# Whole weight units, regrouped gates and the experts' token modulation moved between engines in a two-model network

## The chip, the cores and the metric

The kernel is one launch on one NeuronCore of a Trainium2 chip. The metric is the device time of that launch in microseconds, the median over runs; a profiled execution has a time of its own and a span from its first to its last instruction. Engines are named as the profile names them: PE is TensorE (PEld its weight loads), DVE VectorE, ACT ScalarE, POOL GpSimd, SP SyncE, whose queue (SPq) issues the loads.

## The reference, cut to what matters

Two networks run one after the other on 256 tokens of width 1024 and 256 context tokens. The first has an attention layer and a gated linear recurrence (`hgrn2`), each with a dense feed-forward. The second has two layers, each a mixer followed by a mixture of 32 experts:

```python
# recurrence layer (cut)
q, zf, zb, i, g = jnp.split(a @ w_in, 5, axis=-1)
...                                         # two scans, forward and backward, give o
o = rms_norm(o, o_norm_w)
out = (merge_heads(o) * jax.nn.silu(g)) @ w_o     # g: the gates

# second network, per layer l of 2
x = x + g1 * mixer(...)
h2 = rmsnorm(x, norm_ffn_g[l]) * (1 + sc2) + sh2  # the tokens' modulation ahead of the experts
# layer 0: the 256 context tokens as well (512 rows), layer 1 (the last): 256 rows
x = x + g2 * hier_moe(h2, ...)

def hier_moe(xt, ...):                            # top 2 of 32 experts per token, each of width 512
    ...                                           # group softmax, top_k, weights
    hb = silu(xb @ w1[e]) * (xb @ w3[e])          # xb: the tokens of expert e, gathered
    y[tok] += weights * (hb @ w2[e])
```

All weights are float32. Those of the experts are 2 layers x 32 experts x 6 MiB = 384 MiB.

## The kernel before, in words

Features lie on the partitions (128), tokens on the free axis; `self.X` holds the running tokens as 8 chunks of 128 features. Weights come from DRAM in *units* of 128 rows x 2048 floats (1 MiB; a few are narrower). `raw` (L299) loads a unit on SP's queue as two transfers of 1024 columns each, into two tiles of a ring; the ring of the dense stages has room for 6 units (RING), in the expert stages 7 more are added (`experts`, L270). `fetch` loads units ahead of their use. SP issues in order; a transfer waits until its tile is free.

Dense products run in `linear` (L404): `split_w` cuts a unit into a high and a low part (ACT casts, DVE subtracts), and `mm3` does three products on PE. Work that must fill gaps is stepped in by hand: `step` advances one side chain by one piece after each pair of outputs, `tick` one piece of the background (the `ada` products that make the modulation vectors of later layers).

`hgrn_` (L1109) loops over four pairs of heads. For each it does five products of one unit each: two forget gates, q, the values (`token_major`) and the output gates (`take_g`), and it then appends a side chain, `hg_chain`, of 12 pieces (a preparation, 9 levels of scores, the output, a sum of squares), which is stepped under the products of the next pair of heads; the pieces that are left are done by `finish_side` at the end of that pair. After the loop the last chain is finished with one background tick a piece.

`moe` (L1455) is an expert stage. Layer 0 has 512 tokens and takes 2 experts at a time (G = 2, 64 slots each), layer 1 has 256 tokens and takes 4 (G = 4, 32 slots each; there `whole` is true). Its entry: DVE works out the router's choice in a chain of small operations that ends in `both` (L1550); PE counts positions (`pos`), DVE turns them into keys and one-hot matrices (`gather`, L1616). Meanwhile `turn` (L1474) makes token-major copies of X with the modulation applied: PE multiplies X with `dg` (the identity times the scale A, built on POOL, L1468), and adds a broadcast shift `sb`; for the first three tiles of half 0 ACT applies the token's norm y and POOL adds the shift (L1498), for the others DVE does both (L1501). In layer 0 the copies are split into a high and a low part (ACT L1507, POOL L1508). Half 0 is the first four feature chunks, half 1 the others. `gather.get` multiplies the copies with the one-hots on PE (L1647) and copies the gathered features to SBUF (L1649).

Then, for each group of G experts, `first` (L1654) does the w1 and w3 products (L1668) and `second` the w2 product (L1713); `combine` (L1733, L1734) spreads two groups' results over the tokens. Each feature chunk's product waits for the columns of the units that it reads. At the end of layer 0's stage come the loads of the next dense stage; `pair` (L384) gives high and low tiles from a small pool of their own (`early`) there, and the rest of that pool takes units of layer 1's experts ahead of time.

Of the kernel before, what the change touches and what calls it, by code (L numbers as in the profile page):

```python
# [9 lines left out]
F32 = mybir.dt.float32  # L10
# [233 lines left out]
class Net:  # L244
    def __init__(self, tc, I, out, cat, sat, ctx):
# [5 lines left out]
        self.ring = pool("ring", 2 * self.RING)  # L251
# [3 lines left out]
        self.early = None  # L255
# [13 lines left out]
    @contextmanager  # L269
    def experts(self, name, ck, ring2):  # L270
        tc = self.tc
        with tc.tile_pool(name=f"ck{name}", bufs=ck) as self.ck:
            with tc.tile_pool(name=f"ring{name}", bufs=2 * ring2) as self.ring2:
                with tc.tile_pool(name=f"r{name}", bufs=1) as self.rpool:
                    yield
# [24 lines left out]
    def raw(self, key, pool=None):  # L300
# [4 lines left out]
        n = ap.shape[-1]  # L305
        parts = []
        for i in range(0, n, 1024):
            w = min(n - i, 1024)
            t = (pool or self.ring).tile([P, 1024], F32, tag="raw", name="raw")
            self.nc.sync.dma_start(t[:, :w], ap[..., i : i + w])  # L310
            parts.append(t)
        return lambda lo, hi: parts[lo // 1024][:, lo % 1024 : lo % 1024 + hi - lo]
# [71 lines left out]
    def pair(self, pool=None):  # L384

        if pool:
            t = pool.tile([P, 1024], F32R, tag="raw", name="hl")
            return t[:, :512], t[:, 512:]
# [726 lines left out]
    def hgrn_(self, a, mod, hpool):  # L1115
# [9 lines left out]
        for hp in range(4):  # L1125
            base = hp * 5
            q = self.chunk(name="hq")
            g = self.chunk(name="hg")
# [5 lines left out]

            def take_g(k, ps):
                nc.scalar.activation(g[:, k * S : (k + 1) * S], ps[:, :S], AF.Sigmoid)
                nc.vector.tensor_tensor(g[:, k * S : (k + 1) * S], g[:, k * S : (k + 1) * S], ps[:, :S], op=ALU.mult)
# [309 lines left out]
    def moe(self, l, entry, mod, segs, sl, after):  # L1447
# [16 lines left out]
        dg, sb = {}, {}  # L1464
        for half in range(2):
# [9 lines left out]
        def turn(half):  # L1475

            for _, row in segs:
                ps = self.ps("sb")
# [8 lines left out]
            for t in range(TC):  # L1487
# [14 lines left out]
                if whole:  # L1502
                    hh[2 * t + half] = x
                    continue
# [110 lines left out]
        def gather(kt, base, width):  # L1615
# [19 lines left out]
            def get(i):  # L1635
                while len(xe) <= i:
# [102 lines left out]
        rings = [self.ring] * self.RING + [self.ring2] * (self.ring2.bufs // 2)  # L1739
# [307 lines left out]
```

## Time and profile before

| | |
|---|---|
| median of 3 runs | 2674.04 us (2669.76 to 2677.62) |
| the profiled execution | 2669.05 us, span 2667.2 us |
| PE busy | 2435.3 us, 91% of the span |
| DVE, ACT, POOL busy | 40%, 30%, 9% |
| DMA, mean | 244 GB/s; 409 GB/s in two long stretches |

The page cuts the span in 40 slices of 66.7 us:

```profile
## 2 busy tenths in 40 slices
PE   6999999999999989999998999999989988877775
POOL 1000020101111122111112000000020000000000
PEclk9999999999999999999998999999989998988987
DMA  8158442222532276557613999999934459999996
GB/s 306 64 189 289 171 172 95 95 91 83 209 113 82 80 289 226 181 173 249 237 52 135 386 409 409 408 409 409 409 132 139 147 200 409 409 409 409 409 409 250
```

Each digit is a share in tenths (9 is 90% or more). The dense stages are slices 1 to 21 and 30 to 32, layer 0's experts slices 22 to 29 (from about 1425 to 1946 us), layer 1's experts 33 to the end (from 2170 us). A matmul of two float32 operands is recorded as two instructions. The chain of work that the page follows back from the end breaks off in an empty loop at 2647 us, so the stages are read from windows, timelines and waits.

### The profile page before, as it was taken

The page shows a single profiled execution, that of the slowest core. Times are in us where ns is not written, and L with a number is a line of the kernel's source. Part 1 is how long each engine was busy: PE and PEld are TensorE (multiplying, and loading weights), DVE is VectorE, ACT ScalarE, POOL GpSimd, SP SyncE. Part 2 cuts the span into 40 slices and gives each one's busy share as a digit, 9 for nine tenths or more (in the row PEclk, how much of TensorE's full clock was granted, in tenths as well). Part 3 has the DMA queues.
Part 4 walks back from the last instruction along what each step waited for, and adds up shares of the span by engine and source line. Part 5 has one row for each costly group of instructions (what it writes and reads, how often), then busy time and mean ns, then how long its engine had stood idle before and what let it go on. Part 6 is the DMA issues. An engine that isn't in the chain of part 4 may idle for free. (4 is left out here: it accounts for less than half of the span.)

```text
span 2667.2 us, 35570 instructions
## 1 busy us (share of the span) xinstructions
PE 2435.3 (91%) x13988; PEld 1628.6 (61%) x13988; DVE 1071.7 (40%) x2220; ACT 802.5 (30%) x1430; POOL 239.2 (9%) x217
## 2 busy tenths in 40 slices
PE   6999999999999989999998999999989988877775
PEld 3556678888699958996566544544459762222212
DVE  3456243232566665555664133333344741110102
ACT  4644242222444444445442111111134521000001
POOL 1000020101111122111112000000020000000000
PEclk9999999999999999999998999999989998988987
DMA  8158442222532276557613999999934459999996
GB/s 306 64 189 289 171 172 95 95 91 83 209 113 82 80 289 226 181 173 249 237 52 135 386 409 409 408 409 409 409 132 139 147 200 409 409 409 409 409 409 250
DMA packets 181057, 649.64 MB, mean 244 GB/s; under 512 B 19985, under 2 KB 21137, under 8 KB 180753
## 3 DMA queue, kind: packets, MB, share of 16 engines
q1 hardware_dynamic: 180608, 646.21, 64.6%
q8 instruction: 114, 1.87, 0.3%
q0 software_dynamic: 272, 1.05, 0.1%
q14 instruction: 63, 0.51, 0.1%
HBM read 646.13 MB, written 1.05 MB: 243 GB/s over the span
## 5 line engine op out<-in xcount | busy, mean ns | idle before, releaser
L400 PE MATMUL ps<-h,wh 128*128 128x512 f32 (+1 forms) x1396 | 482.1, 349 | 8.7 <-ACT h L565 7.2
L401 PE MATMUL ps<-l,wh 128*128 128x512 f32 (+1 forms) x1396 | 482.8, 346 | 4.0 <-DVE l L567 3.9
L1668 PE MATMUL w<-raw,xe 128*64 128x512 f32 (+1 forms) x2040 | 416.9, 656 | 74.7 <-DMA raw<-in_moe_w_dram 70.2
L402 PE MATMUL ps<-h,wl 128*128 128x512 f32 (+1 forms) x1396 | 481.6, 346 | 3.1 <-DVE wl L330 3.1
L330 DVE TENSOR_TENSOR wl<-raw,wh 128x1024 fp32r<-128x1024 f32 x254 | 310.7, 1244 | 165.8 <-ACT wh L329 161.9
L329 ACT CAST wh<-raw 128x1024 fp32r<-128x1024 f32 (+1 forms) x258 | 258.1, 1029 | 384.4 <-PE ps L401 300.5
L1668 PEld LDWEIGHTS w<-raw,xe 128*64 128x64 f32 (+1 forms) x2040 | 128.8, 131 | 341.0 <-issue 197.2
L400 PEld LDWEIGHTS ps<-h,wh 128*128 128x128 f32 x1396 | 265.3, 191 | 59.6 <-issue 13.9
L401 PEld LDWEIGHTS ps<-l,wh 128*128 128x128 f32 x1396 | 266.8, 191 | 39.1 <-DVE l L567 6.7
L402 PEld LDWEIGHTS ps<-h,wl 128*128 128x128 f32 x1396 | 266.6, 191 | 38.4 <-DVE wl L330 3.8
L1713 PE MATMUL y<-raw,ut 128*64 128x512 f32 (+1 forms) x1024 | 225.4, 597 | 31.1 <-ACT ut L1687 15.3
L1678 DVE TENSOR_TENSOR u<-u,w 128x512 f32<-128x512 f32 x24 | 16.5, 688 | 436.0 <-PE w L1668 436.0
L1713 PEld LDWEIGHTS y<-raw,ut 128*64 128x64 f32 (+1 forms) x1024 | 65.1, 123 | 171.9 <-issue 107.0
L1724 DVE SCALAR_TENSOR_TENSOR yl<-y,st,yh 128x512 fp32r<-128x512 f32 x48 | 35.5, 750 | 294.3 <-ACT yh L1723 202.5
L583 DVE SCALAR_TENSOR_TENSOR X<-ps,mod,X 128x256 f32<-128x256 f32 x120 | 53.5, 480 | 175.5 <-PE ps L402 175.5
L400 PE MATMUL ps<-uh,wh 128*128 128x512 f32 (+1 forms) x352 | 118.3, 336 | 0.0
L401 PE MATMUL ps<-ul,wh 128*128 128x512 f32 (+1 forms) x352 | 118.3, 336 | 0.0
L402 PE MATMUL ps<-uh,wl 128*128 128x512 f32 (+1 forms) x352 | 118.3, 336 | 0.0
L630 PE MATMUL ada<-raw,cs 128*32 128x512 f32 x768 | 112.3, 606 | 2.7 <-DMA raw<-in_ada_dram 2.6
L964 POOL TENSOR_TENSOR ul<-u,uh 128x512 fp32r<-128x512 f32 (+1 forms) x44 | 74.9, 1702 | 414.4 <-ACT uh L963 414.4
L960 DVE TENSOR_TENSOR u<-u,ps 128x512 f32<-128x512 f32 (+1 forms) x44 | 24.4, 555 | 206.1 <-PE ps L402 199.5
L1723 ACT ACTIVATE yh<-y,st 128x512 fp32r<-128x512 f32 x48 | 32.3, 686 | 237.4 <-PE y L1713 237.0
(372 smaller groups left out, 3498.8 us busy)
## 6 DMA issues: line engine op xcount, KB each, us to landing
raw<-in_moe_w_dram SPq DMA_DIRECT2D x766, 512.0 KB, 10.2
raw<-in_ada_dram SPq DMA_DIRECT2D x192, 512.0 KB, 5.4
raw<-in_ffn_dram SPq DMA_DIRECT2D x128, 512.0 KB, 4.6
raw<-in_hg_in_dram SPq DMA_DIRECT2D x40, 512.0 KB, 4.8
raw<-in_od_in_dram SPq DMA_DIRECT2D x24, 512.0 KB, 9.7
raw<-in_ev_in_dram SPq DMA_DIRECT2D x10, 512.0 KB, 6.3
raw<-in_mla_o_dram SPq DMA_DIRECT2D x8, 512.0 KB, 7.0
raw<-in_hg_o_dram SPq DMA_DIRECT2D x8, 512.0 KB, 9.9
```

What stands on the lines that cost most here:

```text
L329: self.nc.scalar.copy(h[:, c], rc)
L330: eng.tensor_tensor(l[:, c], rc, h[:, c].bitcast(F32), op=ALU.subtract)
L400: mm(out, w[0], a[0], start=start, stop=False)
L401: mm(out, w[0], a[1], start=False, stop=False)
L402: mm(out, w[1], a[0], start=False, stop=stop)
L583: self.nc.vector.scalar_tensor_tensor(x, ps[:, cs], self.m(mod, m, row)[:, k : k + 1], x, op0=ALU.mult, op1=ALU.add)
L630: nc.tensor.matmul(ps[32 * j : 32 * j + 32, :], self.cs[:, blk, k, :], r(j * 512, (j + 1) * 512), start=k == 0, stop=k == NC - 1,)
L964: nc.gpsimd.tensor_tensor(lo[:, :n], u, h[:, :n].bitcast(F32), op=ALU.subtract)
L1668: end = nc.tensor.matmul(ps[x * cap : (x + 1) * cap, :], xk[:, off + x * cap : off + (x + 1) * cap], wc[x], start=k == 0, stop=k == NC - 1,)
L1713: nc.tensor.matmul(ys[nh][x * cap : (x + 1) * cap, :], ut[:, hc * P + x * cap : hc * P + (x + 1) * cap], wc[x], start=hc == 0, stop=hc == 3,)
L1723: ACT.activation(yh[:], ys[nh][:], AF.Copy, scale=sw)
L1724: V.scalar_tensor_tensor(yl[:], ys[nh][:], sw, yh[:].bitcast(F32), op0=ALU.mult, op1=ALU.subtract)
```

## The change

- `raw` loads a unit with one transfer of 2048 columns into one tile; the rings count whole units (6, 7 and 5 tiles of 2048 columns in place of twice as many of 1024). The high and low tiles of `pair` are halves of such a tile.
- In `hgrn_` the gates' four units leave the loop; one `linear` over the four follows it, before the last chain is finished.
- In `moe` with 512 tokens (layer 0): `dg` is built on ACT, four operations of 128 columns a tile, inside `turn`; norm and shift are applied by DVE for every tile, issued after `both` (half 0) or after the one-hots (half 1); the low part of tiles 2 and 3 of half 0 is made on DVE after the one-hots (`late`), the rest stays on POOL.
- In `moe` with 256 tokens (layer 1): X is only transposed, both halves at once, and multiplied by the norm on ACT; there is no `dg`, no `sb`, nothing on POOL. Scale and shift are applied when the gathered features are copied out, ACT and DVE by turns.

```diff
@@ class Net, pools
-        self.ring = pool("ring", 2 * self.RING)
+        self.ring = pool("ring", self.RING)
...
@@ raw
-        n = ap.shape[-1]
-        parts = []
-        for i in range(0, n, 1024):
-            w = min(n - i, 1024)
-            t = (pool or self.ring).tile([P, 1024], F32, tag="raw", name="raw")
-            self.nc.sync.dma_start(t[:, :w], ap[..., i : i + w])
-            parts.append(t)
-        return lambda lo, hi: parts[lo // 1024][:, lo % 1024 : lo % 1024 + hi - lo]
+        t = (pool or self.ring).tile([P, 2048], F32, tag="raw", name="raw")
+        self.nc.sync.dma_start(t[:, : ap.shape[-1]], ap)
+        return lambda lo, hi: t[:, lo:hi]
...
@@ pair
-            t = pool.tile([P, 1024], F32R, tag="raw", name="hl")
+            if not self.halves:
+                t = pool.tile([P, 2048], F32R, tag="raw", name="hl")
+                self.halves = [t[:, 1024:], t[:, :1024]]
+            t = self.halves.pop()
...
@@ hgrn_
-            self.linear([("hg_in", base + 4)], 8, 2, a, lat, take_g)
-            G.append(g)
             self.finish_side()
             self.side.append(self.hg_chain(hp, q, fc, kc, fl, kl, V, O, sums, mk, zero))
+
+        def take_g(k, ps):
+            if k % 2 == 0:
+                G.append(self.chunk(name="hg"))
+            g, ks = G[-1], slice(k % 2 * S, (k % 2 + 1) * S)
+            nc.scalar.activation(g[:, ks], ps[:, :S], AF.Sigmoid)
+            nc.vector.tensor_tensor(g[:, ks], g[:, ks], ps[:, :S], op=ALU.mult)
+
+        self.linear([("hg_in", 5 * hp + 4) for hp in range(4)], 8, 2, a, lat, take_g)
         self.finish_side(1)
...
@@ moe, turn
+            if whole:
+                for i in range(0 if half else 2 * TC):
+                    t, h = divmod(i, 2)
+                    tp = self.ps("htp")
+                    for c in range(4):
+                        x = self.X[:, h * 4 + c, sl.start + t * P : sl.start + (t + 1) * P]
+                        nc.tensor.transpose(tp[:, c * P : (c + 1) * P], x, ident)
+                    x = hh[i] = self.chunk(name="tx")
+                    ACT.activation(x[:], tp[:], AF.Copy, scale=y[:, t : t + 1])
+                return
             for _, row in segs:
                 d = dg[row, half] = self.chunk(name="dg")
-                nc.gpsimd.tensor_tensor(
-                    d[:].rearrange("p (k e) -> p k e", k=4),
-                    ident.unsqueeze(1).broadcast_to([P, 4, P]),
-                    A[:, row * 8 + half * 4 : row * 8 + half * 4 + 4].unsqueeze(2).broadcast_to([P, 4, P]),
-                    op=ALU.mult,
-                )
+                for c in range(4):
+                    k = row * 8 + half * 4 + c
+                    ACT.activation(d[:, c * P : (c + 1) * P], ident, AF.Copy, scale=A[:, k : k + 1])
...
-                if half == 0 and t < 3:
-                    ACT.activation(x[:], tp[:], AF.Copy, scale=y[:, t : t + 1])
-                    nc.gpsimd.tensor_tensor(x[:], x[:], sb[row][:], op=ALU.add)
-                else:
-                    with tc.issue_after(hot_ins[-1] if half else both_ins[-1]):
-                        V.scalar_tensor_tensor(x[:], tp[:], y[:, t : t + 1], sb[row][:], op0=ALU.mult, op1=ALU.add)
+                with tc.issue_after(hot_ins[-1] if half else both_ins[-1]):
+                    V.scalar_tensor_tensor(x[:], tp[:], y[:, t : t + 1], sb[row][:], op0=ALU.mult, op1=ALU.add)
...
-                nc.gpsimd.tensor_tensor(lo[:], x[:], h[:].bitcast(F32), op=ALU.subtract)
+                rest = lambda eng, lo=lo, x=x, h=h: eng.tensor_tensor(lo[:], x[:], h[:].bitcast(F32), op=ALU.subtract)
+                if half or t < 2:
+                    rest(nc.gpsimd)
+                else:
+                    late.append(rest)
...
@@ gather.get
-                    nc.scalar.copy(x[:], ps[:])
+                    if not whole:
+                        ACT.copy(x[:], ps[:])
                     for j in range(per):
-                        xe.append(x[:, j * width : (j + 1) * width])
+                        o, s = (v[:, j * width : (j + 1) * width] for v in (x, ps))
+                        scale, shift = mod_of(len(xe))
+                        if whole and j % 2:
+                            V.tensor_scalar(o, s, scale, shift, op0=ALU.mult, op1=ALU.add)
+                        elif whole:
+                            ACT.activation(o, s, AF.Identity, bias=shift, scale=scale)
+                        xe.append(o)
...
             if g == 0:
+                with tc.issue_after(hot_ins[-1]):
+                    for rest in late:
+                        rest(V)
                 turn(1)
```

## Rows read from the trace of the kernel before

**Rows 1.** Windows: inside layer 0's and layer 1's experts; busy us, granted clock, DMA share, GB/s.

```profile
1500.00:1900.00 400.00, 388.12 (x1976) 196.55 (x1974) 125.91 (x284) 50.38 (x82) 0.00 (x0) 1.00 1.03 409
2210.00:2600.00 390.00, 296.66 (x1519) 96.18 (x1522) 41.95 (x111) 25.28 (x41) 0.00 (x0) 0.90 1.03 409
```

**Rows 2.** Timeline of PE in layer 0: start, us, line, count, [idle before, releaser].

```profile
1712.32 13.95 PE L1668 MATMUL w<-raw,xe 128*64 128x512 f32 x64
...
1771.94 7.89 PE L1668 MATMUL w<-raw,xe 128*64 128x512 f32 x34
...
1785.52 3.65 PE L1668 MATMUL w<-raw,xe 128*64 128x512 f32 x14 [1.47 <-DMA raw<-in_moe_w_dram]
```

**Rows 3.** Waits of PE in layer 1's experts: us in total, times, longest.

```profile
PE w L1668 <- DMA raw<-in_moe_w_dram: 66.7, 47, 2.2
```

**Rows 4.** Page, parts 2, 3, 6: packets by size, instruction queues, two kinds of load.

```profile
DMA packets 181057, 649.64 MB, mean 244 GB/s; under 512 B 19985, under 2 KB 21137, under 8 KB 180753
...
q8 instruction: 114, 1.87, 0.3%
...
q14 instruction: 63, 0.51, 0.1%
...
raw<-in_moe_w_dram SPq DMA_DIRECT2D x766, 512.0 KB, 10.2
...
X<-in_x_dram SPq DMA_DIRECT2D x1, 2048.0 KB, 9.7
```

**Rows 5.** Windows in the first microseconds, while X is being loaded.

```profile
8.00:9.00 1.00, 0.00 (x0) 0.00 (x0) 0.00 (x0) 0.00 (x0) 0.00 (x0) 1.00 0.96 410
...
4.00:9.00 5.00, 0.00 (x0) 0.00 (x0) 0.78 (x4) 0.99 (x2) 0.00 (x0) 1.00 1.03 411
```

**Rows 6.** DVE by line and shape, 1424 to 1442 us: busy, mean ns, idle before.

```profile
L1529 DVE TENSOR_TENSOR r<-eq,r 128x128 f32<-128x128 f32 x2 | 2.3, 1140 | 0.1
L1569 DVE TENSOR_TENSOR tmp<-r,cst 128x128 f32<-128x128 f32 x2 | 1.6, 814 | 0.0
L1537 DVE TENSOR_TENSOR r<-L,r 128x32 f32<-128x32 f32 x4 | 1.6, 461 | 0.0
L1526 DVE TENSOR_TENSOR eq<-r,r 128x128 f32<-128x128 f32 x2 | 1.6, 800 | 0.1
L1527 DVE TENSOR_TENSOR eq<-eq,cst 128x128 f32<-128x128 f32 x2 | 1.5, 756 | 0.0
...
L519 DVE TENSOR_SCALAR rq<-rq 128x4 f32<-128x4 f32 x1 | 1.0, 961 | 0.0
...
L1545 DVE SCALAR_TENSOR_TENSOR r<-r,r 128x128 f32<-128x128 f32 x1 | 0.3, 292 | 0.0
```

**Rows 7.** The same view of ACT, POOL and DVE, 1424 to 1456 us.

```profile
L1508 POOL TENSOR_TENSOR tl<-tx,th 128x512 fp32r<-128x512 f32 x8 | 10.3, 1285 | 11.0 <-ACT th L1507 10.8
...
L1501 DVE SCALAR_TENSOR_TENSOR tx<-htp,rq,sb 128x512 f32<-128x512 f32 x5 | 3.7, 740 | 0.0
...
L1497 ACT ACTIVATE tx<-htp,rq 128x512 f32<-128x512 f32 x3 | 2.1, 684 | 0.3 <-PE htp L1492 0.3
```

**Rows 8.** Waits, 1424 to 1456 us: layer 0's entry on PE.

```profile
PE pos L1554 <- DVE r L1550: 8.7, 1, 8.7
```

**Rows 9.** DVE by line and shape, 2170 to 2182 us: layer 1's entry.

```profile
L1527 DVE TENSOR_TENSOR eq<-eq,cst 128x8 f32<-128x8 f32 x1 | 1.2, 1177 | 0.0
L1529 DVE TENSOR_TENSOR r<-eq,r 128x8 f32<-128x8 f32 x1 | 1.0, 987 | 0.0
```

**Rows 10.** Timeline of PE: layer 1's first product.

```profile
2189.78 3.64 PE L1668 MATMUL w<-raw,xe 128*32 128x512 f32 x32 [0.68 <-ACT xe L1649]
```

**Rows 11.** Window around it: busy us, granted clock, DMA share, GB/s.

```profile
2190.00:2200.00 10.00, 10.00 (x86) 4.27 (x82) 0.00 (x0) 0.59 (x2) 0.00 (x0) 1.00 0.76 265
```

**Rows 12.** Timeline of PE in the recurrence, at the end of a pair of heads.

```profile
811.43 1.95 PE L1051 MATMUL att<-qt,kt 128*128 128x128 f32 x16
```

**Rows 13.** ACT in the recurrence, 720 to 1010 us: by line and shape.

```profile
L1031 ACT COPY qt<-Qf 128x256 f32<-128x256 f32 x32 | 13.4, 419 | 12.5 <-DVE Qf L1019 9.8 <-DVE Qf L1023 2.7
```

More of the change, by code (lines that the diff above doesn't have):

```diff
@@ L254, in __init__ @@
         self.dpool = self.begin.enter_context(tc.tile_pool(name="dpool", bufs=1))
-        self.early = None
+        self.early, self.halves = None, []
         self.ready, self.cut, self.background, self.side, self.due = {}, {}, [], [], []
@@ L272, in experts @@
         with tc.tile_pool(name=f"ck{name}", bufs=ck) as self.ck:
-            with tc.tile_pool(name=f"ring{name}", bufs=2 * ring2) as self.ring2:
+            with tc.tile_pool(name=f"ring{name}", bufs=ring2) as self.ring2:
                 with tc.tile_pool(name=f"r{name}", bufs=1) as self.rpool:
@@ L1127, in hgrn_ @@
             q = self.chunk(name="hq")
-            g = self.chunk(name="hg")
             fc, kc, fl, kl = ([self.chunk(name=nm) for _ in range(2)] for nm in ("fc", "kc", "fl", "kl"))
@@ L1133, in take_q @@
                 nc.scalar.copy(q[:, k * S : (k + 1) * S], ps[:, :S])
-            def take_g(k, ps):
-                nc.scalar.activation(g[:, k * S : (k + 1) * S], ps[:, :S], AF.Sigmoid)
-                nc.vector.tensor_tensor(g[:, k * S : (k + 1) * S], g[:, k * S : (k + 1) * S], ps[:, :S], op=ALU.mult)
             def take_z(d):
@@ L1463, in moe, with turn @@
         ident = self.c("ident")
-        dg, sb = {}, {}
-        for half in range(2):
+        dg, sb, late = {}, {}, []
+        mod_of = lambda k: (A[:, segs[0][1] * 8 + k : segs[0][1] * 8 + k + 1], self.m(mod, 3, segs[0][1])[:, k : k + 1])
+        def turn(half):
+            if whole:
[8 more added lines that the diff above has]
+                return
             for _, row in segs:
                 d = dg[row, half] = self.chunk(name="dg")
-                nc.gpsimd.tensor_tensor(
-                    d[:].rearrange("p (k e) -> p k e", k=4),
-                    ident.unsqueeze(1).broadcast_to([P, 4, P]),
-                    A[:, row * 8 + half * 4 : row * 8 + half * 4 + 4].unsqueeze(2).broadcast_to([P, 4, P]),
-                    op=ALU.mult,
-                )
-        def turn(half):
-            for _, row in segs:
+                for c in range(4):
+                    k = row * 8 + half * 4 + c
+                    ACT.activation(d[:, c * P : (c + 1) * P], ident, AF.Copy, scale=A[:, k : k + 1])
                 ps = self.ps("sb")
@@ L1495, in turn @@
                 x = self.chunk(name="tx")
-                if half == 0 and t < 3:
-                    ACT.activation(x[:], tp[:], AF.Copy, scale=y[:, t : t + 1])
-                    nc.gpsimd.tensor_tensor(x[:], x[:], sb[row][:], op=ALU.add)
-                else:
-                    with tc.issue_after(hot_ins[-1] if half else both_ins[-1]):
-                        V.scalar_tensor_tensor(x[:], tp[:], y[:, t : t + 1], sb[row][:], op0=ALU.mult, op1=ALU.add)
-                if whole:
-                    hh[2 * t + half] = x
-                    continue
+                with tc.issue_after(hot_ins[-1] if half else both_ins[-1]):
+                    V.scalar_tensor_tensor(x[:], tp[:], y[:, t : t + 1], sb[row][:], op0=ALU.mult, op1=ALU.add)
                 h = self.chunk(F32R, name="th")
@@ L1738, in moe @@
         nxt = [0]
-        rings = [self.ring] * self.RING + [self.ring2] * (self.ring2.bufs // 2)
+        rings = [self.ring] * self.RING + [self.ring2] * self.ring2.bufs
         extra = int(self.early is not None)
         if self.early:
-            rings = [self.early] * (self.early.bufs // 2) + rings
+            rings = [self.early] * self.early.bufs + rings
         def static(g):
@@ L1918, in run @@
             r = self.full_rstd([self.X[:, k, al] for k in range(NC)], T)
-        with self.tc.tile_pool(name="early", bufs=2 * self.EARLY) as self.early:
+        with self.tc.tile_pool(name="early", bufs=self.EARLY) as self.early:
             with self.dense("b", 28):
```

## The prediction

> **What bounds the kernel now.** I read the page's slices first, then windows inside the two expert stages, then who PE waits for, and last the timelines of the two entries. The page's slices show PE nearly always busy in the dense stages and a flat 409 GB/s in the two expert stages. In the dense stages PE sets the time and the loads run ahead, so the number of loads there costs nothing. The expert stages differ from each other. In layer 1 the loads run at 409 GB/s throughout while PE is busy 297 us of 390 [rows 1], and PE waits 66.7 us for units in its w products alone [rows 3]: the loads set the time. In layer 0 both are full: PE is busy 388 of 400 us at the same 409 GB/s [rows 1]. There I read PE's timeline. Four experts take PE from 1712.32 to 1771.94, 59.6 us [rows 2]; their 24 units of 1,048,576 bytes take 24 x 2.564 = 61.5 us at 409 GB/s. The loads are 1.9 us a round slower, and the 13 units that are loaded ahead hide this until 1772 us. Then 64 products that took 13.95 us end at 1785.52 + 3.65, after 17.2 us [rows 2]: 3.3 us of waiting, followed by three more such stretches to the stage's end with some 1.8 us each, 8.7 us together. At both entries DVE's routing chain is on the path: PE waits 8.7 us for it in layer 0 [rows 8].
>
> **The change, part by part.** The sums are made against the profiled execution, 2669.05 us (span 2667.2 and 1.9 around it). It lies 5.0 below the median of the runs, which I add at the end.
>
> *Whole units.* A row of a unit in DRAM is 8 KB, and before it was fetched in two pieces of 4 KB. Does a longer row move faster? The only load in this trace with rows over 4 KB is X's, 128 rows of 16 KB. Its rows were not cut: 181057 - 180753 = 304 packets have 8 KB and more, of which 114 + 63 are instruction loads at most, so at least 127 are X's [rows 4]. The rate I take per busy DMA engine, because engines were idle in part: 409 / 1.03 = 397 in the steady stream [rows 1]; while X came in, 411 / 1.03 = 399 over five microseconds, and 410 / 0.96 = 427 in the last one that X fills [rows 5]. So 16 KB rows need 0.5% to 7.0% less engine time. Were this a fixed cost of a packet, 16 KB saves three packets of four and 8 KB two, two thirds of it: 0.3% to 4.7%. Both rows are short and early, neither is nearer to a steady stream, so I take the middle, 2.6%: 420 GB/s, 2.497 us a unit.
>
> [...]
>
> Layer 1: 192 units less 18 loaded ahead, 174 x 2.564 = 446 us, become 174 x 2.497 = 434.4: **-11.6** (-1.3 to -20.9). PE's 76% leaves it room to follow. Layer 0: 24 x 2.497 = 59.9 us against PE's 59.6. The drift falls from 1.9 to 0.3 us a round, some 2 us over the stage, and the stock that lasted 4.4 rounds was worth 4.4 x 1.9 = 8.4. A whole unit takes something from that stock: its first columns are there one half transfer (1.28 us) later, and its tile comes free one half later, 2.6 together. What is left still covers the drift, so PE's waiting of 8.7 us goes nearly away: **-8** (from +1.2, when the rate gains 0.3%, to -8.7); after that PE itself is the bound, and no faster load brings more. At the very end of layer 1 the last w2 unit comes as a whole: 16 more of the products are done after it has landed, at 3.64 / 32 = 0.114 us [rows 10]: **+1.8**. SP issues half as many loads, which nothing waits for. A ring holds as many units as before; a few narrow units take a whole tile, in stages where PE sets the time: nothing.
>
> *Entry of layer 0.* Seven kinds of DVE operations in the chain before `both` stand beside POOL's work, and five of them take two to four times what an operation of their size takes alone: L1529 1.140 us, L1569 0.814, L1526 0.800, L1527 0.756, against 0.292 for L1545 of the same 128x128 [rows 6]. The excess is 2 x (0.848 + 0.522 + 0.508 + 0.464) = 4.7; L1537 and L519, smaller and so bounded by the same 0.292, add 4 x 0.169 + 0.669 = 1.3. After the change POOL has nothing to do before `both`, so the chain is 6.0 us shorter. What comes back: three more tiles on DVE at 0.740 [rows 7] fall into its wait for PE's positions; the two low parts moved to DVE, at most 0.74 each, come between the one-hots and the next tiles, and the first gather needs them. Until now that gather came right behind PE's second half of `turn`, so part of the 1.5 us is hidden there: +1 (0.5 to 1.5). ACT builds `dg` in eight operations of 128 columns a half; a 512-column one takes 0.684 [rows 7], so they take between a quarter and the whole of that, 1.4 to 5.5 us a half. I take them at nothing, since ACT waits for `sb` from PE in that time and the multiplications behind it are needed only after `both`; if that cover is gone, up to 3 us return. POOL's two low parts (1.285 us each [rows 7]) stay ahead of the one-hots' end. Sum **-5** (-1.5 to -5.5). Next in line is then the copy of the gathered features on ACT, behind the casts of half 1. As PE or the loads bound the stage from there on and both start with the first product, what the entry gains is kept.
>
> *Entry of layer 1.* The chain has two such operations, 1.177 and 0.987 us for 128x8 [rows 9]: 1.6 us at least; PE's second half of `turn` ahead of the first gather is gone too, so the first product starts 1.6 to 3.5 us sooner. It is the loads that matter here, which idle (1 - 265/409) x 10 = 3.5 us around that product [rows 11], waiting for it to free a tile. A whole unit is freed at the end of the 32 products, 3.64 us [rows 10], its first half was freed midway, 1.8 sooner. So loading resumes between 0.2 later and 1.7 sooner: **-1**. The copies with scale and shift are split between ACT and DVE, which are nearly idle in that stage.
>
> *Gates.* Each pair's chain loses the gates' product, under which its score levels 7 and 8 ran without a gap (1.95 us for the 16 instructions [rows 12]). What must be ready for them are four copies a level on ACT, 0.419 each [rows 13]: 2 x 4 x 0.419 = 3.35 us a pair, which stands open if nothing else is ready, and nothing if the next pair's first product, whose weights are cut in time, moves in front. Three pairs: 0 to +10; **+3**, nearer to the lower end, as products and chain pieces are interleaved there already. The last chain now runs under the gates' 23 us; the eight background ticks that filled it move to later ticks: nothing.
>
> **Sum.** -11.6 - 8 + 1.8 - 5 - 1 + 3 = -20.8: 2648.2 against the profiled execution, **2653** against the median.
>
> **The rivals.**
> *Rows of 8 KB move no faster* (or the unit is still cut into 4 KB). [...] Against it: X's uncut rows and the last microsecond. Then layer 1 gives -1.3, layer 0 +1.2, the rest stays: +1.2 - 1.3 + 1.8 - 5 - 1 + 3 = -1.3, or 2673. Chance 0.16, no change that can be told.
> *Longer rows move slower.* Twice the bytes are under way at a time, up to 8 transfers of 1 MiB, and an engine is held twice as long by a row. At an unchanged 409 the sum is +2.6 + 1.8 - 5 - 1 + 3 = +1.4. Then both stages are bound by the loads, 174 + 179 units; from 0.019 us a unit more, 406 GB/s, it is slower by over 0.3%. At 400 GB/s: 353 x 0.057 = 20, plus 1.4: 2696. Against it: no window of rows 1 or 5 is below 397 per busy engine. Chance 0.04.
> *The rate rises, but the moved work shows.* All three chains stand open (+10 in place of +3) and ACT's `dg` delays layer 0 (+3): -20.8 + 10 = -11, or 2663. For it: the chain's copies have no other cover by the program's order. Chance 0.12.
> The forecast has 0.68.
>
> **How the numbers follow.** 0.3% of 2674 us, 8 us, is about what a measurement of this kernel tells from no change. Faster: 0.68 + 0.12 = 0.80; same 0.16; slower 0.04. With the best ends, -20.9 - 8.7 + 1.8 - 5.5 - 1.7 + 0 = -35, the time is 2639. The other end of the range takes in the third rival and reaches toward the first: 2670.
>
> **What would show it.** Right: units of 1 MiB and packets of 8 KB, about 420 GB/s in both stages; no wait of w for a load in layer 0, PE's round still 59.6 us; PE's wait for the routing chain in layer 0 down from 8.7 to about 3 us, with no DVE operation of 128x128 over 0.3 us before `both`; layer 1's stream some 12 us shorter. Wrong: 409 GB/s as before (first rival), less (second), new waits of PE for ACT's `qt` or `kt` copies at the ends of pairs or for `dg` (third).

## The result, and the profile after

The median falls from 2674.06 to 2644.32 us (four runs of each; after 2642.53 to 2645.18): 0.9889 of the time before, 95% interval 0.9871 to 0.9906. The prediction, 2653 with a range of 2639 to 2670, holds the time and its sign, but it is 9 us too high. The profiled execution after took 2644.89 us (span 2643.1), 24.2 below that of before.

What the change does to the loads is on the page: half as many packets, one load of 1 MiB for a unit, and in the experts' slices 419 to 420 GB/s. The first line shows all transfers by the size of their packets (of 93495 packets only 16784 are now below 8 KB, against 180753 of 181057 in [rows 4]). The second is the group of layer 0's and 1's products, with the idle time ahead of them. The third is the expert units' loads with size and time to landing.

```profile
DMA packets 93495, 649.52 MB, mean 246 GB/s; under 512 B 10256, under 2 KB 11408, under 8 KB 16784
...
L1679 PE MATMUL w<-raw,xe 128*64 128x512 f32 (+1 forms) x2040 | 406.2, 634 | 76.2 <-DMA raw<-in_moe_w_dram 72.7
...
raw<-in_moe_w_dram SPq DMA_DIRECT2D x383, 1024.0 KB, 19.9
```

Windows inside the two expert stages of the changed kernel, columns as in [rows 1]. The rate is 10 to 11 GB/s higher in both, and PE's share of layer 0 rises from 388.12 to 390.89 of 400 us.

```profile
1490.00:1890.00 400.00, 390.89 (x2003) 198.89 (x2003) 128.72 (x290) 52.20 (x84) 0.00 (x0) 1.00 1.01 419
2190.00:2580.00 390.00, 291.92 (x1565) 99.39 (x1557) 51.47 (x129) 27.29 (x47) 0.00 (x0) 0.93 1.01 420
```

PE's timeline in layer 0, where [rows 2] had the first wait for a unit. The four-expert round is again 1766.32 - 1706.70 = 59.62 us, but the stretch that took 17.2 us takes 13.95 now, and no wait follows.

```profile
1706.70 13.95 PE L1679 MATMUL w<-raw,xe 128*64 128x512 f32 x64
...
1766.32 13.95 PE L1679 MATMUL w<-raw,xe 128*64 128x512 f32 x64
```

At layer 0's entry PE's wait for the routing chain is 2.8 us, against 8.7 [rows 8]. The wait for the gathered features was there before (3.1 us, now 2.4); the one for ACT's `dg` is new:

```profile
PE pos L1558 <- DVE r L1554: 2.8, 1, 2.8
...
PE w L1679 <- ACT xe L1654: 2.4, 1, 2.4
...
PE htp L1499 <- ACT dg L1484: 1.9, 1, 1.9
```

DVE there, by line and shape: the operations that [rows 6] shows at 0.76 to 1.14 us take 0.28 to 0.29.

```profile
L1533 DVE TENSOR_TENSOR r<-eq,r 128x128 f32<-128x128 f32 x2 | 0.6, 292 | 0.1
...
L1573 DVE TENSOR_TENSOR tmp<-r,cst 128x128 f32<-128x128 f32 x2 | 0.6, 282 | 0.0
```

**Where the time went, stage by stage.** I took the start of the same PE product at each boundary in both timelines. The table gives each stage's length less that of before, in us, for the changed kernel and a second set of runs of it, and for eight of the kernels that follow (each is introduced below). The boundaries in the kernel before: the norm ahead of the recurrence at 703.88, the next norm at 1019.14, the router's transposed logits at 1424.85, layer 0's first `w` at 1455.41, the norm behind it at 1950.91, layer 1's logits at 2170.92, its first `w` at 2189.78, the last norm at 2652.08.

| kernel | to 704 | 704-1019 | 1019-1425 | entry 0 | layer 0 | 1951-2171 | entry 1 | layer 1 | end |
|---|---|---|---|---|---|---|---|---|---|
| changed | +6.7 | -6.7 | -1.0 | -4.7 | -6.8 | 0.0 | -2.3 | -10.2 | +1.0 |
| changed, again | +8.9 | -7.7 | -0.7 | -4.4 | -6.7 | -1.0 | -2.3 | -10.0 | +0.9 |
| whole units alone | +8.3 | +1.5 | -0.8 | 0.0 | -8.4 | -1.0 | +0.1 | -10.4 | -0.2 |
| gates alone | +5.4 | -1.7 | +0.1 | -0.3 | -0.4 | +0.3 | +0.1 | +0.2 | 0.0 |
| two transfers | +0.9 | -2.6 | +0.6 | -5.0 | +3.3 | +0.5 | -2.3 | +0.9 | -0.2 |
| one transfer, 4 KB | +6.8 | -6.0 | +0.4 | -4.5 | +2.6 | +0.7 | -2.4 | +1.1 | +0.5 |
| first cast | +4.7 | -6.7 | -0.6 | -4.4 | -6.5 | -1.0 | -2.3 | -9.9 | +0.8 |
| ticks early | +9.0 | +7.6 | -3.7 | -4.9 | -8.1 | +0.3 | -2.3 | -9.4 | +0.9 |
| both mended | -1.5 | -6.6 | +0.4 | -3.6 | -5.6 | +0.1 | -2.3 | -10.2 | +1.0 |
| ticks late | +3.3 | -3.2 | +13.0 | -5.2 | -5.8 | +0.1 | -2.3 | -10.2 | +1.0 |

Two stages went as no term of the sum had it: the start, some 7 us worse, and the recurrence with its output product, some 7 us better. They hide each other in the total.

**The start.** PE's first dense product begins at 46.81 instead of 38.59. The view is PE's timeline, before and after:

```profile
35.93 0.66 PE L643 MATMUL adat<-cst,adae 128*128 128x128 f32 x4 [0.69 <-ACT adae L640]
38.59 0.73 PE L400 MATMUL ps<-h,wh 128*128 128x512 f32 x2 [2.00 <-ACT h L565]
```

```profile
37.54 1.12 PE L641 MATMUL adat<-cst,adae 128*128 128x128 f32 x4 [0.71 <-ACT adae L638]
46.81 0.80 PE L398 MATMUL ps<-h,wh 128*128 128x512 f32 x1 [8.16 <-ACT wh L324]
```

It waits 8.16 us for ACT's cast of the first weights, 6.2 more than it waited there before; another 1.6 of the delay were lost ahead of that (37.54 against 35.93). ACT's timeline shows that cast as the first operation behind `adae` before, and as the one behind thirteen operations of the modulation after, with ACT busy from 39.17 almost throughout:

```profile
35.77 1.05 ACT L329 CAST wh<-raw 128x1024 fp32r<-128x1024 f32 x1
```

```profile
39.17 0.60 ACT L555 ACTIVATE t<-t,mod,modA 128x256 f32<-128x256 f32 x1 [1.68 <-DVE modA L527]
...
45.73 1.03 ACT L324 CAST wh<-raw 128x1024 fp32r<-128x1024 f32 x1
```

**The recurrence.** PE has 4.1 us of new waits at the ends of two pairs. But the windows (before, then after; the recurrence with its chain, and the attention) show 64 products fewer in the first stretch and 60 more in the second, which is nevertheless 1.0 us shorter: its granted clock is 1.00 in place of 0.97, and PE idles 5.5 us of it instead of 8.9. The first stretch is 4.2 us shorter; the other 2.4 us of the stage's gain lie in the output product behind it.

```profile
PE att L1049 <- ACT kt L1032: 4.1, 4, 1.1
```

```profile
703.88:979.08 275.20, 265.91 (x1840) 229.84 (x1836) 177.92 (x350) 132.30 (x274) 58.63 (x67) 0.99 0.42 147
...
1222.97:1386.34 163.37, 154.44 (x893) 99.58 (x889) 101.53 (x243) 81.31 (x169) 30.49 (x44) 0.97 0.51 183
```

```profile
710.57:981.54 270.97, 259.13 (x1776) 228.84 (x1772) 179.94 (x348) 133.43 (x276) 59.28 (x67) 0.99 0.33 120
...
1222.99:1385.36 162.37, 156.90 (x953) 98.31 (x950) 103.63 (x247) 81.64 (x170) 30.75 (x44) 1.00 0.63 233
```

PE's waits in the attention show which ones went, before and then after. The longest single one was not for a softmax result but for ACT's copy `adae` at the end of a bank of background products:

```profile
PE adat L643 <- ACT adae L640: 3.1, 1, 3.1
PE tp L714 <- ACT p L704: 3.1, 3, 2.4
```

```profile
PE tp L712 <- ACT p L702: 1.8, 1, 1.8
...
PE adat L641 <- ACT adae L638: 0.7, 1, 0.7
```

### The profile page after: what moved, and what is told of

Read it like the earlier page. It is cut to its first block, busy times and chain, and to the rows that moved or that the text cites. A ratio compares the mean times of both kernels' runs of the same rounds, so it can differ in the third digit from the quotient of the medians.

```text
span 2643.1 us, 34246 instructions
## 1 busy us (share of the span) xinstructions
PE 2411.1 (91%) x13956; PEld 1622.6 (61%) x13956; DVE 1077.7 (41%) x2243; ACT 807.1 (31%) x1447; POOL 224.4 (8%) x204
## 2 busy tenths in 40 slices
DMA packets 93495, 649.52 MB, mean 246 GB/s; under 512 B 10256, under 2 KB 11408, under 8 KB 16784
## 5 line engine op out<-in xcount | busy, mean ns | idle before, releaser
L1679 PE MATMUL w<-raw,xe 128*64 128x512 f32 (+1 forms) x2040 | 406.2, 634 | 76.2 <-DMA raw<-in_moe_w_dram 72.7
```

The lines of the kernel that those rows point to most:

```text
L1679: end = nc.tensor.matmul(ps[x * cap : (x + 1) * cap, :], xk[:, off + x * cap : off + (x + 1) * cap], wc[x], start=k == 0, stop=k == NC - 1,)
```

## The experiments

**Is it the row, the transfer or the tile?** My theory: the 8 KB row. Rivals: the transfer of 1 MiB (half as many transfers and completions), or something in the whole tiles. The first kernel has the loads' part of the change and nothing else (`raw`, the rings, `pair`).

> The kernel before with the whole units alone: one 1 MiB transfer a unit, whole tiles; gates and modulation as before. If the loads' part does what the traces suggest, the stream of layer 1 runs at 420 GB/s and gives 10 us, PE's waits for units in layer 0 vanish and give 7, and the start is some 7 us later, because the first weights come as a whole unit and ACT's cast of them stands behind the modulation in its queue: -10, about 2664 in the median. The rival is that the start has another cause (the gates or the modulation's order): then the first dense product starts at 39 us as before, and the time is 17 below, 2657.

2657.31 us, 0.9943 of before (0.9927 to 0.9960). The median is the rival's figure, but the trace decides against it: the start is 8.3 later, with the same wait of PE, 8.15 us. Both expert stages gain at least what they gain in the whole change (-8.4 and -10.4; some 1.7 of the 8.4, by an estimate of 10 x 0.17, would be the granted clock of layer 0's first 10 us, 1.00 where the kernel before and the changed one have 0.83), the entries nothing. So the loads' part brings both the gain in the experts and the loss at the start.

The second kernel cuts each unit's load in two again, into the same whole tile:

```
-        self.nc.sync.dma_start(t[:, : ap.shape[-1]], ap)
+        n = ap.shape[-1]
+        for i in range(0, n, 1024):
+            c = slice(i, min(i + 1024, n))
+            self.nc.sync.dma_start(t[:, c], ap[..., c])
```

> The changed kernel, but every unit is fetched by two transfers of 1024 columns into its whole tile: rows of 4 KB, slots and all else as changed. If the length of a row sets the rate, both expert stages fall back to 409 GB/s: layer 1 gives back 10 us and layer 0 about 7. The first half unit lands some 2.5 us earlier and its cast stands ahead of the modulation in ACT's queue, so the start gains 7: together 10 slower than the changed kernel, 2654. If the whole tile or anything but the row were behind the rate, it stays 420 and the time is 7 below the changed kernel, 2637.

2665.44 us, 0.9981 (0.9971 to 0.9991). The third keeps one transfer of 1 MiB for an expert unit but has the unit in DRAM as two blocks of 1024 columns, so that a row is 4 KB:

```
-        a[f"moe_{n}"] = np.ascontiguousarray(w.reshape(2, 32, 2, P, 2048))
+        a[f"moe_{n}"] = np.ascontiguousarray(w.reshape(2, 32, 2, P, 2, 1024).transpose(0, 1, 2, 4, 3, 5))
...
+            self.nc.sync.dma_start(t[:].rearrange("p (h c) -> p h c", h=2), ap.rearrange("h p c -> p h c"))
```

> The changed kernel, but the experts' units lie in DRAM as two blocks of 1024 columns and come by one transfer of 1 MiB with 4 KB rows; the other units keep their 8 KB rows. If the length of a row sets the rate: 409 GB/s in both expert stages, packets of 4 KB, 17 us slower than the changed kernel, 2661. If the size of the transfer sets it (half as many transfers and half as many completions): 420 GB/s and 2644.

2666.96 us, 0.9984 (0.9974 to 0.9993). The windows of the two kernels, layer 0 and layer 1 of each:

```profile
1490.00:1890.00 400.00, 387.34 (x1970) 195.22 (x1970) 126.91 (x288) 50.34 (x83) 0.00 (x0) 1.00 1.03 409
2210.00:2600.00 390.00, 295.54 (x1490) 97.47 (x1479) 48.77 (x121) 25.19 (x42) 0.00 (x0) 0.90 1.03 409
```

```profile
1500.00:1900.00 400.00, 387.72 (x1970) 196.13 (x1970) 126.45 (x284) 50.57 (x82) 0.00 (x0) 1.00 1.03 409
2210.00:2600.00 390.00, 287.68 (x1498) 96.18 (x1494) 48.81 (x121) 25.31 (x42) 0.00 (x0) 0.93 1.03 409
```

409 in all four. Transfers of 512 KB and of 1 MiB ran at the same rate with rows of 4 KB, and the whole tile changed nothing: what separates these 409 from the 419 to 420 of the changed kernel is the row's length. The two kernels' totals missed my figures (2654 and 2661). In both, layer 0 came out some 3 us worse than before and layer 1 some 1 us, and not level. Layer 0's loss fits the 2.6 us which the prediction charged a whole tile for being filled and freed later; what splits it I haven't tried. With two transfers the recurrence, too, is 4.1 us worse than in the changed kernel: PE waits 6.7 us there for ACT's `rh`, as in the kernel with the gates alone below. Two transfers also give the start back: first dense product at 39.93, wait 2.00.

**What the start costs, and why.** Theory: the place of the first cast in ACT's queue. Rival: the whole unit lands later. Here I only fix the first cast ahead of the modulation in ACT's queue (the lines in `split_w` that note this cast as `self.first` are left out).

```
-            a = self.modulated(m0, "norm1_0", 0, 1, whole, al, r=r)
+            self.first, key = None, ("mla_in", 0)
+            self.cut[key] = self.split_w(key)
+            with self.tc.issue_after(self.first):
+                a = self.modulated(m0, "norm1_0", 0, 1, whole, al, r=r)
```

> The changed kernel once more, to stand beside the three that follow: 0.989 of the kernel before.

> The changed kernel with one thing more: ACT's modulation of the first features is issued behind ACT's first cast of the first dense weights, instead of ahead of it. If the 8.2 us that PE waits at 38.7 us come from the order in ACT's queue, the cast starts when the whole unit has landed, near 39 us, and PE's first dense product near 41.5 in place of 46.8: 5 us sooner, of which 4 or more are still there at 700 us, 2640. If they come from the whole unit's later landing, the product still starts at 45 us or later: 2644.

The changed kernel again: 2645.10 us, 0.9889 (0.9872 to 0.9905). With the first cast ahead: 2640.48, 0.9870 (0.9853 to 0.9886), 4.6 less on the same chip. Its cast (ACT's timeline) and first dense product (PE's):

```profile
39.42 1.99 ACT L324 CAST wh<-raw 128x1024 fp32r<-128x1024 f32 x2 [1.51 <-DMA raw<-in_mla_in_dram]
```

```profile
42.28 1.22 PE L400 MATMUL ps<-h,wh 128*128 128x512 f32 x2 [3.20 <-ACT h L565]
```

The cast begins when the unit has landed, 6 us sooner than in the changed kernel. PE's wait is 3.2 us, against 2.0 with two transfers and 8.2 with the cast behind: of the 6.2 us the queue's order accounts for 5.0, and the later landing, with the modulation now behind the cast, for at most 1.2.

> The changed kernel, but the three units of the first dense weights come by two transfers of 1024 columns each, into whole tiles. The order that is worked out at build time then has the first cast ahead of the modulation, and the first half lands 2.5 us sooner than the whole: first dense product near 40 us as in the kernel with two transfers everywhere (39.9), PE's wait before it 2.0 in place of 8.2, and 6.7 us less at 700 us: 2638. If the start is lost to something else (the constants' whole tile, the units loaded ahead), the wait stays: 2644.

2643.51 us, 0.9882 (0.9865 to 0.9899); only these three units are cut, by `w = 1024 if key[0] == "mla_in" else n` in `raw`. First product at 42.52, wait 3.44; at 704 us it stands 3.9 better than the changed kernel's second set, but 1.6 of that is lost again in the recurrence and 2.6 in the attention (165.2 us against 162.7; in its first 30 us the granted clock is 0.89 against 1.00). The figure of 2638 was too good. The start also varies by itself: the kernel with the gates alone has the start of before, word for word, and its first dense product was at 42.45. Over the profiles, eight kernels with an early first cast (the one before among them) reach the norm at 704 us between 1.5 sooner and 5.4 later than before, six with the late one between 6.7 and 9.0 later. The means are 2.3 and 7.9: the late cast costs some 5.6 us, of which the medians of the two kernels on one chip show 4.6.

**The gates and the ticks.** The gates' part of the diff alone (`hgrn_`), on the kernel before:

> The kernel before with the regrouped gates alone. The prediction on record gives +3 (0 to +10). The trace after the change suggests otherwise: the stretch from the recurrence's start (704 us) to 1386 us is 7.7 us shorter, with 4.1 us of new waits of the score products for ACT's copies, but eight background ticks moved from the recurrence into the attention of 1223 to 1386 us, where they fill PE's waits and keep the granted clock at 1.00 (0.97 before). If that is the gates' doing, the time is 2666 (-8). If it came from the whole units in those stages instead, the gates alone cost the 4 us of new waits: 2678.

2671.91 us, 0.9992 (0.9981 to 1.0003): no change. The 4.1 us of waits are there, the 64 products have moved too, but the recurrence with its output gains 1.7 us and not 6.7. The difference is one wait: PE waits 6.7 us for ACT's `rh` at the recurrence's end, and 2.1 in the changed kernel. ACT's timeline shows why, here with the gates alone and then changed:

```profile
976.51 1.04 ACT L329 CAST wh<-raw 128x1024 fp32r<-128x1024 f32 x1 [1.29 <-DMA raw<-in_hg_o_dram]
977.57 1.28 ACT L468 ACT_TABLE_LOAD   x1
...
984.06 0.62 ACT L679 CAST rh<-r 128x512 fp32r<-128x512 f32 x1 [1.74 <-DVE r L471]
```

```profile
976.66 1.28 ACT L466 ACT_TABLE_LOAD   x1
...
978.76 1.99 ACT L324 CAST wh<-raw 128x1024 fp32r<-128x1024 f32 x2 [0.17 <-DMA raw<-in_hg_o_dram]
980.87 0.62 ACT L677 CAST rh<-r 128x512 fp32r<-128x512 f32 x1
```

With half loads the cast of the next weights stands ahead of the norm's last activation (L468) and waits for its load there; with whole units it stands behind it (L466). The late activation makes 2.3 us of the 4.6; as much again goes to DVE, where the low parts `wl` of the weights cast so early stand between the three last steps of the norm. It is the start's mechanism with the other sign.

Then the ticks. Theory: the eight background ticks (one bank, 64 products) that left the recurrence are the gain. I put eight back, in one block ahead of the last chain's remaining pieces and not, as before, one after each piece:

```
+        self.tick(8)
         self.finish_side(1)
         R = self.rows_rstd(sums, 3)
```

> The changed kernel with eight background ticks (one bank of a later block's modulation, 64 products and about 9 us of PE) put back into the recurrence, as before. If their move is what gave 7 us there, the recurrence is 9 us longer, and the attention of 1223 to 1386 us loses their 8 us of products but gets back PE's waits for the softmax (3.1 and 1.6 us) and the lower granted clock (0.97): 6 slower than the changed kernel, 2650. If their place is without effect: 2644.

2657.93 us, 0.9941 (0.9924 to 0.9957): 12.8 above the changed kernel, twice what I expected. The same two stretches:

```profile
712.91:994.40 281.49, 266.21 (x1829) 231.20 (x1826) 179.53 (x350) 131.94 (x274) 59.35 (x67) 0.99 0.38 140
...
1239.00:1399.21 160.21, 151.50 (x892) 97.75 (x889) 101.32 (x243) 81.05 (x169) 31.96 (x44) 0.99 0.49 185
```

The recurrence has 53 products more than in the changed kernel and is 281.49 - 270.97 = 10.5 us longer; the attention has 61 fewer and is only 162.37 - 160.21 = 2.2 shorter. So the bank costs some 10 us in the recurrence and about 2 in the attention, 8 net. Of the 10, PE's busy time is 266.21 - 259.13 = 7.1; the rest is idle time, 2.3 of it waits for the bank's own loads. Behind it the output product is 3.8 us longer (41.4 against 37.6): PE is busy 1.9 longer, at a granted clock of 0.84 against 0.91, and idles 1.9 longer, since it waits 4.8 us for ACT's cast of the weights, which in this kernel stands behind the four casts of `h`. So the 12.8 us are not the ticks' own price alone. PE's waits, in the recurrence and then from 700 to 1425 us:

```profile
PE ada L628 <- DMA raw<-in_ada_dram: 2.3, 2, 2.0
```

```profile
PE ps L398 <- ACT wh L324: 4.8, 1, 4.8
```

Against the kernel before, the stretch from 704 to 1425 us is 7.6 - 3.7 = 3.9 us longer. That is near the 4.1 us of waits for `kt`, but as it holds these other waits too, it doesn't show by itself what the regrouping costs if the ticks stay.

The opposite, no ticks in the last chain (with the first cast ahead):

```
-        self.finish_side(1)
+        self.finish_side()
         R = self.rows_rstd(sums, 3)
```

> The changed kernel with the first cast ahead of the modulation (2640.5 so far), and the last pair's chain without background ticks: the ticks that stood there (some 2 units of 8 products and the rest of a bank) move into the attention as well. If a tick is worth the wait that it lies under, and not more, the recurrence loses their products, gets back waits of about 1 us at the last chain's levels, and the attention, where PE idles only 5.5 of 162 us now, has to add most of them to its time: no gain, 2640 to 2645. If ticks in the recurrence cost their whole time whatever lies beside them, as the eight that were put back did, the time falls by 4 or more: 2636 or less.

2656.66 us, 0.9938 (0.9914 to 0.9962), 16 above the kernel with the first cast: worse than either figure. The recurrence has 32 products fewer and is yet 275.39 - 270.95 = 4.4 us longer, with a wait of 6.9 us for ACT's copy `adae` at the end of a bank, and the attention is 174.81 - 162.78 = 12.0 us longer than with the first cast alone, most of it a wait for the same copy. In ACT's queue it stands behind the norm's last cast in the one place and behind the casts of the next weights and features in the other. So this run doesn't decide between its two figures: what it shows is the price of a bank that ends at such a place. PE's waits, in the recurrence and then from 1230 us on:

```profile
PE adat L643 <- ACT adae L640: 6.9, 1, 6.9
```

```profile
PE adat L643 <- ACT adae L640: 10.5, 2, 9.8
```

**The entry of layer 0.** One part undone: `dg` on POOL again.

```
-                for c in range(4):
-                    k = row * 8 + half * 4 + c
-                    ACT.activation(d[:, c * P : (c + 1) * P], ident, AF.Copy, scale=A[:, k : k + 1])
+                nc.gpsimd.tensor_tensor(d[:]..., ident..., A[:, row * 8 + half * 4 : ...]..., op=ALU.mult)
```

> The changed kernel with one part of the change undone: the diagonals `dg` of layer 0 are built by POOL again, all else as changed. If DVE's operations are slowed by a POOL operation beside them, the two that fall under the first half's `dg` (L519 and the first L521-type of the rsqrt) take 0.96 us again in place of 0.16, PE's wait for the routing chain grows from 2.8 us by 1.6, and the second half's `dg` (2 us) slows some one-hots: the first product of layer 0 is 1.5 to 3 later, 2647. If ACT's `dg` costs as much where it stands now (PE waits 1.9 us for it in the second half), the two cancel: 2645.

2645.59 us, 0.9905 (0.9884 to 0.9926): no difference. The premise did not come about: only two diagonals instead of four are built at the start, and POOL is through with them at 1422.65 + 2.04 = 1424.69, before the operations that had been slowed; the chain's wait on PE stays at 2.9 us. The later ones do fall beside DVE. POOL's timeline, then DVE's:

```profile
1422.65 2.04 POOL L1482 TENSOR_TENSOR dg<-cst,modA 128x512 f32<-128x512 f32 x2 [50.09 <-PE s L2013]
...
1438.36 2.04 POOL L1482 TENSOR_TENSOR dg<-cst,modA 128x512 f32<-128x512 f32 x2
```

```profile
1436.71 0.16 DVE L1603 TENSOR_SCALAR r<-r 128x4 f32<-128x4 f32 x1
...
1439.41 1.01 DVE L1603 TENSOR_SCALAR r<-r 128x4 f32<-128x4 f32 x1
```

The same line takes 0.16 us with POOL idle and 1.01 with POOL busy, and ends at 1440.42, just as POOL does (1438.36 + 2.04 = 1440.40). That POOL's other operations slowed the chain before the change is read from such overlaps and from [rows 6]; no run puts only them back.

Next, ACT's diagonals of the second half moved into its idle 5.6 us in the first half's `turn`, with the first cast ahead:

```
                 ACT.copy(sb[row][:], ps[:])
+            if half == 0:
+                for _, row in segs:
+                    diagonals(row, 1)
             for t in range(TC):
```

> The changed kernel with the first cast ahead of the modulation (as in the run on the first cast, 4.6 below the changed kernel) and with ACT's diagonals of the second half issued in the first half's `turn`, where ACT idles for 5.6 us while the routing chain runs. If PE's wait of 1.9 us for `dg` was on the path of layer 0's entry, the first product is up to 1.9 sooner and, PE being the bound of that stage, 1.9 is kept: 2639. If the gather's one-hots come no sooner than before, only the first cast counts: 2640.5.

2641.24 us, 0.9892 (0.9869 to 0.9915): 4.4 below the run with `dg` on POOL, in the same set, which is what the first cast alone gave, and no more. PE's wait of 1.9 us for `dg` is gone, and the wait for the gathered features takes its place (4.7 instead of 2.4):

```profile
PE w L1688 <- ACT xe L1663: 4.7, 1, 4.7
```

Last, background ticks at each pair's end on top of that (`finish_side(1)` in the loop of `hgrn_` for `finish_side()`):

> As the run with both mended, and in addition the end of each pair's chain takes a background tick at each step, which fall beside the four waits of 1.0 us that the regrouped gates opened. If the waits are filled, 4.1 us of PE's waits for `kt` go and two ticks a pair, some 1.1 us each, come from the stretches behind: at best 4 less than with both mended, 2635; if the ticks only take the place of others that lay under waits later, no gain or up to 3 more.

2653.49 us, 0.9937 (0.9912 to 0.9962), 12 more than without them and worse than any figure I had. The waits for `kt` are gone, but the recurrence is 290.04 - 271.05 = 19.0 us longer than with both mended: it has 95 products more, 15.6 us of PE's busy time, and another long wait for the copy at a bank's end, behind the norm in ACT's queue (PE's waits there; 1.2 us with both mended):

```profile
PE adat L643 <- ACT adae L640: 11.9, 3, 9.5
```

Filling four waits of 1.0 us with ticks was no bargain here.

The best version is the changed kernel with its first cast ahead of the modulation: 2640.5 against 2645.1 us.

## Why the prediction was right in sign and range, and 9 us too high

*The rate.* The step that carried most, 420 GB/s for 8 KB rows, is exact, and its assumption (a fixed cost of a packet) fits what was measured. The exactness is in part luck: 2.6% was the middle of 0.3% to 4.7%, taken because neither of two short rows was nearer. The evidence for the assumption: in the packets' records of the trace the median is 161 ns for 4096 bytes before and 313 for 8192 after, against 322 for two, and 611 for the 16384 of X's rows in both, against 644 for four: 9 and 11 ns for each packet saved. The price at which rivals one and two would have decided, 409 or less, was seen only in the kernels with 4 KB rows.

*Layer 1.* -11.6 + 1.8 = -9.8 predicted, -10.2 measured. The +1.8 was no cost: PE's last stretch of `y` products behind the last wait is 20 products in 3.62 us in both timelines, so before the change, too, most of the last unit's products came after it had landed. That leaves the -11.6 too large by 1.4, for which no run here shows the reason.

*Layer 0.* -8 predicted, -6.8 measured. The waits for units are gone and the round is 59.6 us, as foretold. Of the 8.7 us that I read as waiting, the last 1.8 were none: the stretch at the stage's end, split by the combination's products, is there unchanged after. I had counted four stretches by their length, and should have looked for the releaser in each.

*Entry of layer 0.* -5 predicted, -4.7 (again -4.4) measured. The chain shrank more than my 6.0: from the logits to PE's positions it is 1433.21 - 1423.87 = 9.3 us instead of 16.8 (PE waits 8.7 of them, [rows 8]), 7.4 less, and 2.7 came back, not 1. My 6.0 had left out one operation, L521 (0.96 us beside POOL at 1426.44, 0.16 later in the same chain). `dg` was not hidden as I had it, since PE waits 1.9 us for it, but that wait isn't on the path: with it removed the product starts no sooner. What is late next is the copy of the gathered features, as the prediction said.

*Entry of layer 1.* -1 predicted, -2.3 in every kernel that has that part. My bound of -1.7 was too narrow: it held the loads' resumption to be the limit, worked out from the time at which a unit is freed. The gain is kept: this entry and layer 1 together give -12.5, against -10.3 with whole units alone.

*Gates.* Their own price was about right: +3 predicted, within 0 to +10, and 4.1 us of waits for `kt` measured, at two pairs' ends (2.1 us each, not 3.35) and not at the third. The step that failed is the clause behind it, "the eight background ticks that filled it move to later ticks: nothing". By the run that puts eight back they were worth some 8 us, 10.5 in the recurrence less 2.2 in the attention. I had looked for the cover of the ticks where they came from and not for the idle time where they would go: with the 61 products PE idles 5.5 us of the attention, without them 8.7. A second thing that no term had is where the bank ends and the next weights are cast in ACT's queue; between two kernels with the same ticks it made 4.6 us at the recurrence's end (6.7 against 2.1 of waiting for `rh`), and in the attention a wait of 3.1 us for `adae` before is 0.7 after. How much of the gain of some 7 us is the one and how much the other, no run here splits cleanly.

*The start.* "A few narrow units take a whole tile ...: nothing" looked at the ring and left out that a 1 MiB load also moves the time at which the first weights can be cast, and with it the order in ACT's queue: some 5.6 us by the means over the profiles.

*From the profile to the median.* I added the 5.0 us by which the profiled execution before lay below the median. Most of that may be the start of the kernel before, which is early in that execution (first dense product at 38.59; 42.45 in the kernel that shares its code). The changed kernel's profiled execution lies 0.6 above its median. So of the 9 us by which the prediction is too high, 24.2 - 20.8 = 3.4 are terms of the sum (the recurrence and the start nearly cancel), and the rest is this offset. The hit is thus in part luck: two terms of 6 to 8 us with opposite signs were missing.

Rival three (moved work shows) came true in part: the gates' waits opened, but 4.1 us of them and not 10, and the ticks outweighed them.

What stays open is why the start varies by up to 7 us between the profiles of kernels with an early first cast. The granted clock of 20 to 30 us was 0.83 in the profile before and 0.66 in that of the gates alone, but also 0.66 with two transfers, where the first dense product came at 39.93; so this clock alone doesn't explain it.

## What to carry to other kernels

When a stream of loads sets the time, try a longer row in DRAM before a larger transfer: here 8 KB rows gave 2.7% more than 4 KB rows, which ran alike in transfers of 512 KB and of 1 MiB. The first weights, landing as a whole unit, had their cast behind thirteen operations in ACT's queue, and PE waited 8.2 us there in place of 2.0, so read the queues' order at every point where a load is awaited, above all at the start. Background work cost about its whole time in a full stretch and little where PE idled (one bank some 10 us in the recurrence and about 2 in the attention, where PE idled 8.7 us without it), so price a tick at the place to which it moves, not only at the one that it leaves; and find where the copy at the end of its bank then stands in its engine's queue: in two of the three runs that moved ticks PE waited 9.5 us and more for one such copy.

## What the runs showed of the hardware that I had not expected

A row of 8 KB took 313 ns per packet against 2 x 161 ns for two of 4 KB, 2.9% more, and the rate of the whole stream followed (420 and 409 GB/s, 2.7%); a transfer of 1 MiB instead of 512 KB was worth nothing at the same row of 4 KB (409 and 409). A DVE operation beside a POOL operation lasted until that one ended: TENSOR_SCALAR on 128x4 took 0.16 us alone and 1.01 beside POOL's `dg`, both ending within 0.02 us. A TENSOR_REDUCE there was not slowed: in the kernel before one on 128x128 took 0.29 us at 1434.67, inside a POOL operation of 1.31 us that began at 1434.45. And moving 60 products into a stretch of 163 us made it 1.0 us shorter in the changed kernel, where PE's idle time fell from 8.9 to 5.5 us and the granted clock rose from 0.97 to 1.00. The run that took them out again was at 0.99 and 160.2 us, so the clock isn't shown to hang on them.
